# Down projection of a hybrid decoder step: the second of the two products with one weight block per step is computed third of seven instead of sixth

## The chip, the cores and the metric

The kernel runs on one core of a Trainium2 chip. The metric is the device time of one execution in microseconds, as the median of several runs. A core has PE for matmuls (its weight loads are listed as PEld), DVE and POOL for elementwise work, ACT for activations and copies, and SP, which here issues DMAs. PE adds up in eight PSUM banks.

## The reference, cut to what matters

The reference is one layer of a decoder: adaLN modulation, a gated DeltaNet branch and a sliding-window attention branch, and a gated feed-forward block, for 1024 prompt tokens and 8 single-token samples, all in float32. The change touches the last product, before the final norm:

```python
gc = _causal_dwconv(gate_ext, lp['ffn_conv_w'], L) + lp['ffn_conv_b']
x = x + gt2 * ((jax.nn.silu(gc) * up) @ lp['w_ffn_down'])
...
y_prompt = _rmsnorm(xp, final_norm_w)
y_sample = _rmsnorm(xs, final_norm_w)
```

The activations are (1032 tokens, 2816), `w_ffn_down` is (2816, 1024).

## The kernel before, in words

The kernel goes through the layer in stages; `second_half` (L1904) ends with `ffn_gate_up`, eleven times, and then `ffn_down` (L1726), which also does the final norm. The float32 operands of a product are split into a high and a low part, and `mm3` (L178, lines L180 to L182) makes three matmuls of each block product.

**Seven products.** `ffn_down` cuts activations, weights and output into two by two blocks and multiplies them with seven block products in place of eight, after the manner of Strassen. Each product runs over `G` = 11 steps of 128 rows, 77 steps in all. A step multiplies one activation block (128 x 516, from the scratch tensor `xd` in DRAM) with one weight block (128 x 512) into eight banks (two token halves by four column tiles), 24 matmuls in all. `made` says what a product's weight is made of: products 5 and 2 take one block of `w_ffn_down`, the other five take the sum or difference of two, which POOL computes (L1755).

**Chains.** `chains` gives the order of the products. The products of one tuple add into the same banks. After each product `take` (L1783) has ACT copy the eight banks to SBUF (L1786); PE's next product starts in the first bank once that is copied. The copies lie in a ring of eight slots and are added, times the gate, to the residual `x1` by `add_gated` on DVE (L1472, with L1476 and L1477 for the eight samples); `home` lists where each copy goes: two places, hence 16 additions, for products 5, 3, 1 and 2, and one place, hence 8, for 4 and 7. Product 6 is last, outside this loop, and is interleaved with the final norm.

**Loads.** `fetch` (L1742) issues the loads of a step on SP: a weight block (L1751), for a two-block product the other block into `ws` (L1754, three buffers), and the activation block (L1756). They land in one of five raw buffers: three of the pool `raw`, and two halves of `bmh0` (listed as `bmh`) for steps 3 and 4 of every five. `part` (L1759) splits a raw buffer: ACT writes the high part (L129), DVE the low part (L130); with the latter the raw buffer is free (a half of `bmh0` only together with the other half). The 13 places for split operands, `tags`, are used in turn, so step 39 lies in the same place as steps 0, 13 and 26; a place is free when PE has done the step that used it.

**Order.** `fetch_to` lets the splits run up to 13 steps ahead of PE, and loads four or five further. In the last six steps of each chain's last product it starts loads but no splits. Within these bounds a scheduler in the framework sets the order on each engine; each engine works through its own queue in that order.

Of the kernel before, what the change touches and what calls it, by code (L numbers as in the profile page):

```python
# [64 lines left out]
class Step:  # L65
# [1660 lines left out]
    def ffn_down(self, pool, psum):  # L1726
# [4 lines left out]
        made = {5: (2, (1, 1)), 3: (5, (0, 1), (1, 1), ALU.subtract), 4: (6, (1, 0), (0, 0), ALU.subtract),  # L1731
                7: (4, (1, 0), (1, 1), ALU.add), 1: (0, (0, 0), (1, 1), ALU.add), 2: (1, (0, 0)),
                6: (3, (0, 0), (0, 1), ALU.add)}
        chains = ((5, 3), (4, 7), (1,), (2,), (6,))
        home = {5: ((0, 0, -1), (1, 1, -1)), 3: ((1, 0, 1), (1, 1, 1)), 4: ((0, 1, 1),), 7: ((0, 0, 1),),
                1: ((0, 0, 1), (1, 1, 1)), 2: ((0, 1, 1), (1, 1, -1)), 6: ((1, 1, 1),)}
        steps = [(i, g) for c in chains for i in c for g in range(G)]
# [334 lines left out]
```

## Time and profile before

| what | value |
|---|---|
| median of 3 runs | 2083.78 us (2079.47 to 2090.38) |
| span of the profiled execution | 2084.4 us |
| PE busy over the span | 97% |
| HBM read and written | 212.93 MB, 62.51 MB |
| loads of `ffn_down`: `w_ffn_down` into `ws` | 55 of 256 KB |
| first copies after products 5, 3, 4 in this execution | 1862.8, 1895.17, 1933.32 us |

The profiled execution has no time listed beside its span. A row of the windows has the wall time of a stretch, then the busy time and number of instructions of each engine in it, then the clock granted to PE as a share of full speed, the mean busy share of the DMA engines, and GB/s. In a timeline a row starts with the start and duration in microseconds; the brackets at its end have the engine's idle time before it and what ended it. In the rows of waits, the total, the number and the longest follow the names.

### The profile page before, as it was taken

Reading aid. Unit: us, or ns where it says so; the run is one execution under the profiler, and the core shown is the slowest. Engines: PE = TensorE matmul, PEld = TensorE weight load, DVE = VectorE, ACT = ScalarE, POOL = GpSimd, SP = SyncE. Lnnn points to the kernel's source line nnn. Section 1 sums busy time; section 2 is a strip of 40 time slices with the busy share of each in tenths; the row PEclk is TensorE's granted clock in tenths of the full one; section 3 lists DMA queues with packets and bytes.
Section 4 is the critical chain, followed back from the end, with each engine's and each line's share of the span. In section 5 each row is a group of like instructions: output and inputs, shape, how many; then the busy total and the mean of one; then the engine's idle time right before and its main releaser. Section 6 shows DMA issues by size and latency. Waiting matters only on the chain.

```text
span 2084.4 us, 41297 instructions
## 1 busy us (share of the span) xinstructions
PE 2012.7 (97%) x16245; PEld 1910.2 (92%) x16245; DVE 1347.8 (65%) x2714; ACT 900.2 (43%) x2233; POOL 520.2 (25%) x594
## 2 busy tenths in 40 slices
PE   7999998999999999989989999999999999999897
PEld 4987877799999999989989999999999999999897
DVE  5755768473655647656544675578876776767756
ACT  4664545433344243432342542354444444534443
POOL 2000000121321221201111000005575466446421
PEclk9999999999999999999999999999999999999999
DMA  8256443331332322312275855323333333488862
GB/s 300 62 144 210 135 167 116 117 94 51 80 80 61 73 72 52 89 42 62 63 223 172 285 186 163 112 63 97 105 91 112 102 92 112 136 305 266 291 215 94
DMA packets 301887, 275.75 MB, mean 132 GB/s; under 512 B 59730, under 2 KB 248111, under 8 KB 301676
## 3 DMA queue, kind: packets, MB, share of 16 engines
q1 hardware_dynamic: 295642, 252.14, 39.6%
q0 software_dynamic: 5552, 20.37, 2.8%
q8 instruction: 127, 2.08, 0.4%
q14 instruction: 68, 0.56, 0.1%
q10 hardware_dynamic: 498, 0.61, 0.1%
HBM read 212.93 MB, written 62.51 MB: 132 GB/s over the span
## 4 chain that ended last, share of the span: by engine, by line
PE 83%; DVE 5%; DMA 5%; ACT 3%; issue 1%; SPq 1%; POOL 1%; DVEq 0%; POOLq 0%; ACTq 0%
PE mm L180 19%; PE mm L181 18%; PE mm L182 18%; PE wv L180 3%; PE wv L182 3%; PE wv L181 3%; PE wy L182 2%; PE wy L180 2%; PE wy L181 2%; PE pv L652 1%; PE pt L190 1%; PE tp L190 1%; DVE x L1472 1%; PE mm L264 1%; PE rc L954 1%
## 5 line engine op out<-in xcount | busy, mean ns | idle before, releaser
L180 PE MATMUL mm<-b1h,wh 128*128 128x384 f32 (+1 forms) x1520 | 496.9, 328 | 3.7 <-ACT gt L1294 1.6
L181 PE MATMUL mm<-b1l,wh 128*128 128x384 f32 (+1 forms) x1520 | 489.3, 323 | 0.0
L182 PE MATMUL mm<-b1h,wl 128*128 128x384 f32 (+1 forms) x1520 | 488.0, 323 | 0.3 <-DVE wl L130 0.3
L180 PEld LDWEIGHTS mm<-b1h,wh 128*128 128x128 f32 x1520 | 286.7, 189 | 12.4 <-issue 4.6
L181 PEld LDWEIGHTS mm<-b1l,wh 128*128 128x128 f32 x1520 | 287.1, 189 | 4.4 <-issue 3.1
L182 PEld LDWEIGHTS mm<-b1h,wl 128*128 128x128 f32 x1520 | 286.3, 189 | 3.9 <-issue 2.8
L129 ACT ACTIVATE wh<-raw 128x1024 fp32r<-128x1024 f32 x83 | 87.0, 1049 | 122.4 <-PE mm L181 70.2
L130 DVE TENSOR_TENSOR wl<-raw,wh 128x1024 fp32r<-128x1024 f32 x82 | 101.0, 1233 | 57.2 <-ACT wh L129 55.1
L181 PE MATMUL mm<-pk,w 128*128 128x260 f32 (+1 forms) x440 | 124.8, 284 | 1.1 <-DVE pk L130 1.1
L180 PE MATMUL mm<-pk,w 128*128 128x260 f32 (+1 forms) x440 | 124.8, 284 | 0.0
L182 PE MATMUL mm<-pk,w 128*128 128x260 f32 (+1 forms) x440 | 124.5, 283 | 0.0
L130 DVE TENSOR_TENSOR w<-ws,w 128x512 fp32r<-128x512 f32 x88 | 78.0, 886 | 36.9 <-ACT w L129 36.7
L1626 ACT COPY bml<-mm 128x256 f32<-128x256 f32 (+1 forms) x132 | 48.9, 371 | 100.6 <-PE mm L182 96.7
L180 PE MATMUL mm<-bmh,w 128*128 128x260 f32 (+1 forms) x320 | 90.3, 282 | 0.0
L182 PE MATMUL mm<-bmh,w 128*128 128x260 f32 (+1 forms) x320 | 90.1, 282 | 0.0
L1681 DVE SCALAR_TENSOR_TENSOR fa<-fz,fcw,fa 128x512 f32<-128x512 f32 x88 | 75.2, 874 | 18.2 <-ACT fa L1679 17.9
L180 PE MATMUL mm<-b2h,wh 128*128 128x384 f32 (+1 forms) x256 | 83.2, 328 | 2.9 <-ACT wh L129 2.8
L181 PEld LDWEIGHTS mm<-pk,w 128*128 128x128 f32 x440 | 83.2, 189 | 1.3 <-DVE pk L130 1.3
L181 PE MATMUL mm<-b2l,wh 128*128 128x384 f32 (+1 forms) x256 | 83.6, 327 | 0.4 <-DVE b2l L130 0.4
L180 PEld LDWEIGHTS mm<-pk,w 128*128 128x128 f32 x440 | 83.2, 189 | 0.2 <-ACT bml L1626 0.2
L182 PEld LDWEIGHTS mm<-pk,w 128*128 128x128 f32 x440 | 83.4, 190 | 0.0
L182 PE MATMUL mm<-b2h,wl 128*128 128x384 f32 (+1 forms) x256 | 82.8, 326 | 0.0
(645 smaller groups left out, 5886.2 us busy)
## 6 DMA issues: line engine op xcount, KB each, us to landing
raw<-in_w_in_dram SPq DMA_DIRECT2D x59, 512.0 KB
ws<-in_w_ffn_down_dram SPq DMA_DIRECT2D x55, 256.0 KB
raw<-xd SPq DMA_DIRECT2D x47, 258.0 KB
raw<-in_w_ffn_down_dram SPq DMA_DIRECT2D x47, 256.0 KB
raw<-in_w_ffn_gate_dram SPq DMA_DIRECT2D x22, 512.0 KB
raw<-in_w_ffn_up_dram SPq DMA_DIRECT2D x22, 512.0 KB
qst<-in_w_mod_dram SPq DMA_DIRECT2D x16, 512.0 KB
raw<-in_w_mod_dram SPq DMA_DIRECT2D x16, 512.0 KB
```

The costliest lines, as they stand in the source:

```text
L129: self.nc.scalar.activation(hi, x, AF.Copy)
L130: (eng or self.nc.vector).tensor_tensor(lo, x, hi.bitcast(F32), op=ALU.subtract)
L180: mm(ps, whi, xhi, start=first, stop=False, **kw)
L181: mm(ps, whi, xlo, start=False, stop=False, **kw)
L182: self.last_mm = mm(ps, wlo, xhi, start=False, stop=last, **kw).ins
L190: self.nc.tensor.transpose(out, in_, self.ident[:p, :p])
L264: nc.tensor.matmul(ps[32 * j:32 * j + 32], self.cT[:, k0 + j, :], ws[j // 2][:, j % 2, :], start=k0 == 0, stop=k0 > 0)
L652: nc.tensor.matmul(pv[64 * r:64 * r + 64], V[:, n - back, ch], ps[:, r::2, :], start=back == 0, stop=back == (n > 0))
L954: yield step(nc.tensor.matmul(ds, kd[:, n, :], s, start=True, stop=True))
L1472: nc.vector.scalar_tensor_tensor(x[:, :np_], ps[:, :np_], by[:, j, 8:9], x[:, :np_], op0=ALU.mult, op1=ALU.add)
L1626: self.last_copy = nc.scalar.copy(r[p, i], x[p])
L1681: nc.vector.scalar_tensor_tensor(ai[:, c:e], zi[:, j + c:j + e], col(j), ai[:, c:e], op0=ALU.mult, op1=ALU.add)
```

## The change

One line: product 2 moves from the fourth place in `chains` to the second. It stays a chain of its own.

```diff
@@ -1731,7 +1731,7 @@
         made = {5: (2, (1, 1)), 3: (5, (0, 1), (1, 1), ALU.subtract), 4: (6, (1, 0), (0, 0), ALU.subtract),
                 7: (4, (1, 0), (1, 1), ALU.add), 1: (0, (0, 0), (1, 1), ALU.add), 2: (1, (0, 0)),
                 6: (3, (0, 0), (0, 1), ALU.add)}
-        chains = ((5, 3), (4, 7), (1,), (2,), (6,))
+        chains = ((5, 3), (2,), (4, 7), (1,), (6,))
```

The order of the products is now 5, 3, 2, 4, 7, 1, 6. Steps 22 to 32 are product 2, 33 to 43 product 4, 44 to 54 product 7, 55 to 65 product 1; before, they were 4, 7, 1 and 2. Numbers behind the names in the rows below are the program's; the place's name gives the step.

POOL's queue at the end of product 3's subtractions, before: `raw_2848` belongs to step 21, the next rows to steps 22 to 25.

```order
L1755 TENSOR_TENSOR raw_2848_21399<-raw_2848_21399,ws_2849_21401 128x512
L1755 TENSOR_TENSOR raw_2851_21433<-raw_2851_21433,ws_2852_21435 128x512
L1755 TENSOR_TENSOR bmh0_2854_21475<-bmh0_2854_21475,ws_2855_21477 128x512
L1755 TENSOR_TENSOR bmh0_2854_21475<-bmh0_2854_21475,ws_2857_21510 128x512
L1755 TENSOR_TENSOR raw_2859_21541<-raw_2859_21541,ws_2860_21543 128x512
```

The same place in POOL's queue now: behind step 21 come steps 33 to 36.

```order
L1755 TENSOR_TENSOR raw_2848_21399<-raw_2848_21399,ws_2849_21401 128x512
L1755 TENSOR_TENSOR bmh0_2883_21839<-bmh0_2883_21839,ws_2884_21841 128x512
L1755 TENSOR_TENSOR bmh0_2883_21839<-bmh0_2883_21839,ws_2886_21849 128x512
L1755 TENSOR_TENSOR raw_2888_21880<-raw_2888_21880,ws_2889_21882 128x512
L1755 TENSOR_TENSOR raw_2891_21913<-raw_2891_21913,ws_2892_21915 128x512
```

For steps 22 to 32 POOL now has no instruction of this loop.

ACT's queue at the copies after product 4, before: `bmh3_2910` is the place of step 38, `bmh2_2912` of step 39, `bml0_2915` of step 40; product 4 ends with step 32.

```order
L129 ACTIVATE bmh3_2910_22022<-bmh0_2908_22016 128x1028
L129 ACTIVATE bmh2_2912_22056<-bmh0_2908_22016 128x1028
L1786 COPY bml3_2334_15602<-mm_2881_21849 128x256
L1786 COPY bml3_2334_15602<-wv_2882_21850 128x260
L129 ACTIVATE bml0_2915_22091<-raw_2913_22085 128x1028
L1786 COPY bml3_2334_15602<-wy_2883_21851 128x256
```

The copies after product 4 in ACT's queue now: `bmh3_2951` is the place of step 51, `bmh2_2955` of step 52; product 4 ends with step 43.

```order
L129 ACTIVATE bmh3_2951_22475<-raw_2949_22469 128x1028
L1786 COPY bml3_2334_15602<-mm_2911_22215 128x256
L1786 COPY bml3_2334_15602<-wv_2912_22216 128x260
L1786 COPY bml3_2334_15602<-wy_2913_22217 128x256
L1786 COPY bml3_2334_15602<-mm_2914_22218 128x260
L1786 COPY bml3_2334_15602<-wv_2915_22219 128x256
L129 ACTIVATE bmh2_2955_22513<-raw_2953_22507 128x1028
```

The first copy stood behind the split of the seventh step after product 4's last and now stands behind that of the eighth.

DVE's queue around the low parts of steps 38 and 39, before: the additions behind them are product 4's.

```order
L130 TENSOR_TENSOR bmh3_2910_22022<-bmh0_2908_22016,bmh3_2910_22022 128x1028
L130 TENSOR_TENSOR bmh2_2912_22056<-bmh0_2908_22016,bmh2_2912_22056 128x1028
L1472 SCALAR_TENSOR_TENSOR x1_0_2332_15597<-bml3_2334_15602,mT_125,x1_0_2332_15597 128x256
L1472 SCALAR_TENSOR_TENSOR x1_0_2332_15597<-bml3_2334_15602,mT_125,x1_0_2332_15597 128x252
L1476 TENSOR_TENSOR gtmp_2940_22378<-bml3_2334_15602,mT_125 128x8
```

The low part of step 38 in DVE's queue now, with the first of product 2's additions; sixteen L1472 rows in all stand ahead of the low part of step 39.

```order
L130 TENSOR_TENSOR bmh3_2899_21989<-bmh0_2897_21983,bmh3_2899_21989 128x1028
L1472 SCALAR_TENSOR_TENSOR x1_0_2332_15597<-bml3_2334_15602,mT_125,x1_0_2332_15597 128x256
L1472 SCALAR_TENSOR_TENSOR x1_4_2810_21062<-bml3_2334_15602,less_2807_21058,x1_4_2810_21062 128x256
L1472 SCALAR_TENSOR_TENSOR x1_0_2332_15597<-bml3_2334_15602,mT_125,x1_0_2332_15597 128x252
L1476 TENSOR_TENSOR gtmp_2937_22353<-bml3_2334_15602,mT_125 128x8
L1472 SCALAR_TENSOR_TENSOR x1_4_2810_21062<-bml3_2334_15602,less_2807_21058,x1_4_2810_21062 128x252
```

Both halves of `bmh0` that steps 38 and 39 use become free only after these additions.

## The prediction

> **What bounds the kernel now.** I read the page first, then PE's waits over the down projection, then windows around the one long wait, then the timelines of ACT, DVE, SP and POOL backwards from it. A step is one entry of `steps`; before the change product 5 is steps 0 to 10, product 3 is 11 to 21, product 4 is 22 to 32.
>
> ```profile
> span 2084.4 us, 41297 instructions
> ...
> PE 2012.7 (97%) x16245; PEld 1910.2 (92%) x16245; DVE 1347.8 (65%) x2714; ACT 900.2 (43%) x2233; POOL 520.2 (25%) x594
> ```
>
> PE is the bound and keeps all its matmuls, so time can only come from stretches where PE waits or runs slowly. PE's waits from 1780 us on:
>
> ```profile
> PE mm L180 <- ACT bml L1786: 5.6, 1, 5.6
> PE wv L190 <- DVE x L1477: 1.0, 1, 1.0
> ...
> PE wv L190 <- DVE raw L1896: 0.5, 1, 0.5
> ```
>
> One wait stands out; the others lie in the closing norm. Windows cut at it and at the closing norm (wall, then busy time and count of PE, PEld, DVE, ACT, POOL, then granted clock, DMA share, GB/s):
>
> ```profile
> 1928.16:1933.72 5.56, 0.00 (x1) 0.00 (x1) 3.28 (x3) 2.43 (x4) 3.56 (x3) 0.92 1.03 369
> 1933.72:1939.62 5.90, 5.90 (x27) 5.90 (x28) 5.87 (x7) 4.86 (x10) 3.52 (x4) 0.50 0.97 322
> 1939.62:1945.52 5.90, 5.90 (x52) 5.90 (x51) 5.90 (x11) 2.14 (x2) 2.69 (x3) 1.00 0.75 251
> 2045.42:2048.83 3.41, 1.82 (x14) 1.22 (x13) 3.33 (x10) 1.35 (x4) 0.89 (x2) 1.00 0.21 83
> 2048.83:2052.24 3.41, 3.41 (x18) 3.09 (x17) 2.64 (x15) 1.40 (x5) 1.10 (x2) 0.50 0.58 228
> ```
>
> The wait costs twice: 5.56 us of nothing, then 5.90 us at a clock of 0.50 (27 matmuls where the next 5.90 us hold 52), which is 2.95 us of lost work. Together 8.5 us: all that this place can give. Who made PE wait stands in ACT's timeline:
>
> ```profile
> 1928.87 1.06 ACT L129 ACTIVATE bmh<-bmh 128x1028 fp32r<-128x1028 f32 x1 [1.15 <-POOL bmh L1755]
> 1932.35 1.06 ACT L129 ACTIVATE bmh<-bmh 128x1028 fp32r<-128x1028 f32 x1 [2.42 <-POOL bmh L1755]
> 1933.32 0.35 ACT L1786 COPY bml<-mm 128x256 f32<-128x256 f32 x1
> ...
> 1936.40 1.11 ACT L129 ACTIVATE bml<-raw 128x1028 fp32r<-128x1028 f32 x1
> ```
>
> The L129 at 1932.35 is the split of step 39 (the room after step 38's, and so on: the one at 1936.40 is step 41's). It waits for POOL's subtraction, which waits for data; behind it in ACT's queue stand the copies L1786 that empty product 4's banks; and product 7 adds into those same banks, so PE stands until the first copy. The operands of step 39 itself are not needed for another six steps.
>
> Why was the data late? DMA had a hole shortly before (share 0.32), and the timelines of DVE and SP say why:
>
> ```profile
> 1910.00:1915.00 5.00, 5.00 (x45) 5.00 (x44) 5.00 (x8) 0.17 (x1) 0.00 (x0) 1.00 0.32 64
> ```
>
> ```profile
> 1896.77 2.70 DVE L1472 SCALAR_TENSOR_TENSOR x<-bml,mT,x 128x256 f32<-128x256 f32 x4
> ...
> 1902.25 1.22 DVE L130 TENSOR_TENSOR bml<-raw,bml 128x1028 fp32r<-128x1028 f32 x1
> ...
> 1909.83 1.22 DVE L130 TENSOR_TENSOR bml<-bmh,bml 128x1028 fp32r<-128x1028 f32 x1
> 1910.97 1.21 DVE L130 TENSOR_TENSOR bmh<-bmh,bmh 128x1028 fp32r<-128x1028 f32 x1
> ```
>
> ```profile
> 1905.43 1.77 SPq L1754 DMA_DIRECT2D ws<-in_w_ffn_down_dram  x2
> 1912.21 0.33 SPq L1751 DMA_DIRECT2D bmh<-in_w_ffn_down_dram  x1
> ...
> 1915.42 0.38 SPq L1754 DMA_DIRECT2D ws<-in_w_ffn_down_dram  x1
> ```
>
> Product 3's 16 additions (L1472) fill DVE from 1896.77 to 1909.83. Behind them wait the L130 of steps 28 and 29; these free the `bmh0` buffer, and only then, at 1912.21, can SP issue step 33. I call such a row of 16 additions a burst. From that issue to the end of step 41's split are 1937.5 - 1912.2 = 25.3 us.
>
> **The change part by part.** Matmuls, bytes, subtractions and additions keep their number; the 22 loads of product 2 pass in SP's queue ahead of the loads of products 4, 7 and 1, whose 33 subtractions move back by 11 steps in POOL's queue. What changes is what runs beside each burst. The same burst with and without POOL, and its DVE rows where POOL rests (now product 1's burst):
>
> ```profile
> 1896.77:1909.83 13.06, 13.06 (x112) 13.06 (x111) 13.06 (x24) 6.52 (x10) 7.15 (x5) 1.00 0.76 257
> 1997.42:2004.00 6.58, 6.58 (x58) 6.58 (x57) 6.58 (x20) 6.58 (x12) 0.00 (x0) 1.00 0.00 0
> ```
>
> ```profile
> 1997.42 1.68 DVE L1472 SCALAR_TENSOR_TENSOR x<-bml,mT,x 128x256 f32<-128x256 f32 x4 [10.33 <-ACT bml L1786]
> ...
> 2004.00 1.22 DVE L130 TENSOR_TENSOR pk<-raw,pk 128x1028 fp32r<-128x1028 f32 x1
> ```
>
> Beside five subtractions the burst takes 13.06 us, of which one L130 is 1.1 us: 11.9 us. Without POOL it takes 6.6 us. So a subtraction inside a burst costs it 5.3/5 = 1.06 us.
>
> Step 1, product 3's burst. Steps 22 to 32 now have one weight block, so POOL has nothing between steps 21 and 33, and the copies have no late split before them. The clock of PE is read from the last matmuls of steps 21 and 32 and from the first copy:
>
> ```profile
> 1896.42 0.28 PE L182 MATMUL nr<-pk 128*128 128x260 f32 x1
> ```
>
> ```profile
> 1927.88 0.28 PE L182 MATMUL nr<-pk 128*128 128x260 f32 x1
> 1933.72 0.58 PE L180 MATMUL mm<-pk 128*128 128x256 f32 x1 [5.56 <-ACT bml L1786]
> ```
>
> ```profile
> 1895.17 0.35 ACT L1786 COPY bml<-mm 128x256 f32<-128x256 f32 x1
> ```
>
> Eleven steps take 31.5 us, one 2.86. The first bank of a step has its last of three matmuls (0.12 us apart, 0.28 long) done 0.52 us into the step, 2.3 before its end, so a free copy starts near 1894.2 instead of 1895.17, and additions near 1894.6. Burst over: 1894.6 + 6.6 = 1901.2; two L130 at 1.14 us: step 33 issued at 1903.5, 8.7 us earlier than now. If the rest follows as it did, step 38's split ends at 1929.9 - 8.7 = 1921.2, well before the copies after product 2 (1925.7), ahead of which it now stands. That boundary costs nothing.
>
> Step 2, the new burst. Product 2's 16 additions now fall between the L130 of steps 38 and 39, where product 4's eight stood. They start near 1926.2. POOL's subtractions for steps 41 and 42 are
>
> ```profile
> 1934.59 1.46 POOL L1755 TENSOR_TENSOR raw<-raw,ws 128x512 f32<-128x512 f32 x1 [0.77 <-DMA raw<-in_w_ffn_down_dram]
> 1936.50 1.37 POOL L1755 TENSOR_TENSOR raw<-raw,ws 128x512 f32<-128x512 f32 x1 [0.46 <-DMA ws<-in_w_ffn_down_dram]
> ```
>
> and 8.7 us earlier they fall at 1925.9 and 1927.8, inside the burst. It takes 6.6 + 2 x 1.06 = 8.7 us, to 1934.9; step 39's L130 ends at 1936.1, and SP then issues step 43.
>
> Step 3, product 4's copies. They now stand behind the split of step 51, eight steps past 43, as 41 is past 33: 25.3 us, less one 256 KB block (0.7 us at 369 GB/s) because three blocks are fetched ahead instead of two. The split ends at 1936.1 + 24.6 = 1960.7, the first copy at 1961.0. PE finishes product 4 at 1928.0 + 31.5 = 1959.5. It waits 1.5 us. Bounds: a burst free of POOL, none; five subtractions in it, 1.5 + 3 x 1.06 = 4.7 us.
>
> Step 4, the slow clock behind the wait. In the closing norm PE idled 1.6 of 3.41 us, no single wait over 1.0 us, and the next 3.41 us ran at 0.50: 1.7 us lost. I charge the new wait that much. The Trainium skill (TensorE: Matmul & The Clock Gate, "What's actually happening") says that the clock halves after an idle window of about 3.4 us; by that rule a wait of 1.5 us costs no clock, and the forecast would be 1.7 us lower. The closing norm's row disagrees, since it was half busy there.
>
> Step 5, the closing stretch. Product 1's 16 additions stand where product 2's stood. They have four pairs of the small sample operations (L1476, L1477) instead of eight, and they touch columns 0 to 255, which the first transposes read. I count zero: at best the 1.5 us of L190 waits above go.
>
> Sum: 5.56 + 2.95 goes, 1.5 + 1.7 comes: -5.3 us. The profiled execution (2084.4) lies 0.6 us above the median 2083.78, so 2078.5 us against the median.
>
> **The rivals.** *The wait vanishes*: burst 2 meets no subtraction, or the loads run slightly faster; 2083.8 - 8.5 = 2075.3 us. For it: 1.5 us is all that is missing. Against it: DMA was saturated (1.03 and 0.97) while steps 34 to 41 came in.
>
> *A short wait leaves the clock alone*: 2078.5 - 1.7 = 2076.8 us. For it: the 5.56 us window reads 0.92, so the clock fell only in its last 0.9 us, some 4.7 us into the wait. Against it: the closing norm. The page's rule above is this rival.
>
> *The wait only moves*: burst 2 runs as dense with subtractions as product 3's did. Then 4.7 + 2.95 = 7.65 us stands against 8.5: 2082.9 us. For it: a 16-addition burst before the unpaused copies is just what is there now. Against it: the 8.7 us won at burst 1.
>
> *Slower*: the longer row of two-block steps, 33 to 76 without a light product between, loads more slowly than steps 33 to 41 did. The rows of steps 43 and 49:
>
> ```profile
> 1940.43 1.06 ACT L129 ACTIVATE pk<-bmh 128x1028 fp32r<-128x1028 f32 x1 [1.47 <-POOL bmh L1755]
> ...
> 1958.37 1.06 ACT L129 ACTIVATE pk<-bmh 128x1028 fp32r<-128x1028 f32 x1 [0.17 <-POOL bmh L1755]
> ```
>
> That is 17.94/6 = 2.99 us a step, where 33 to 41 took about 2.3. Eight steps at 0.68 more add 5.4 us; with a dense burst the wait is 4.7 + 5.4 = 10.1, and with 2.95 of slow clock 13.05 us against 8.5: 2088.3 us. It decides once step 51's split ends 4.1 us later than I have it (the old wait of 5.56 again). Against it: eight additions lay in that stretch, and none do in the new one.
>
> **How the numbers follow.** The shrunken wait has 0.42, the same with the clock left alone 0.12, the vanished one 0.20, the moved one 0.14, slower 0.12. The likeliest gives 2078.5 us. The range reaches from the vanished wait with the L190 waits gone too (2075.3 - 1.5 = 2073.8, taken as 2073.5) to just short of the slow rival, 2087. 0.5%, 10.4 us, is about what a measurement of this kernel can tell from no change. No rival alone passes it; the three runs scatter from 2079.47 to 2090.38, so part of the vanished wait falls beyond it (0.15 with what I have not seen), and part of the slow rival (0.07). The rest, 0.78, is within it.
>
> **What would show it.** Product 3's burst without subtractions at about 6.6 us; step 33 issued near 1903.5; no PE wait after product 2; a second burst of 7 to 9 us; one PE wait on L1786, now after product 4 near 1959.5 and under 5 us; at most one 3.4 us window at 0.50 behind it. I am wrong if PE waits after product 2, if the wait at product 4 exceeds 5.6 us, or if time moves in the closing stretch by more than 1.5 us.

## The result and the profile after

The changed kernel takes 2079.41 us in the median of 22 runs (2075.34 to 2088.55); the kernel before, run beside it, takes 2086.67 us (2077.44 to 2094.03, 22 runs). The ratio is 0.9971 with a 95% interval of 0.9959 to 0.9983, which is 6.0 us of 2086.67 (3.5 to 8.6); the two medians alone lie 7.3 us apart. The forecast was 5.3 us. One run of a later kernel (product 2 fifth) took 3917.54 us, for a cause that stays open, and is not in its ratio. The matmuls are all kept, as the page of the changed kernel shows:

```profile
span 2077.9 us, 41299 instructions
...
PE 2011.2 (97%) x16245; PEld 1908.0 (92%) x16245; DVE 1353.8 (65%) x2714; ACT 900.6 (43%) x2233; POOL 521.6 (25%) x594
```

The span is 6.5 us shorter. How far the change itself goes is better read from the first copy after product 5, ahead of which nothing is changed, to PE's last matmul. The windows of this stretch (wall, then busy time and count of PE, PEld, DVE, ACT, POOL, then clock, DMA share, GB/s), in the kernel before:

```profile
1862.80:2076.73 213.93, 205.45 (x1680) 203.21 (x1678) 154.16 (x239) 89.89 (x147) 84.83 (x57) 0.98 0.67 229
```

and in the changed kernel:

```profile
1864.23:2070.17 205.94, 201.34 (x1680) 199.29 (x1678) 157.08 (x239) 90.75 (x147) 86.67 (x57) 1.00 0.69 237
```

The same 1680 matmuls take 8.0 us less: PE idles 4.6 us instead of 8.5, and is busy 4.1 us less, because none of it runs at a lower clock. The stretch starts 1.4 us later in this execution, which has to be taken off where times are compared with the prediction. PE's waits from 1780 us on in the changed kernel:

```profile
PE mm L180 <- ACT bml L1786: 1.9, 1, 1.9
PE wy L190 <- ACT ws L1873: 1.0, 1, 1.0
PE wv L190 <- DVE raw L1896: 1.0, 1, 1.0
PE mm L181 <- DVE pk L130: 0.5, 1, 0.5
```

The wait of 5.6 us is now one of 1.9, still on L1786, and the closing norm's waits are the size they were. The stretches on which the prediction rested, as windows: the burst after product 3, the burst after product 2, and three of 3.41 us at the wait.

```profile
1896.10:1902.69 6.59, 6.59 (x57) 6.59 (x57) 6.59 (x20) 6.59 (x12) 0.00 (x0) 1.00 0.63 230
1927.59:1936.31 8.72, 8.72 (x75) 8.72 (x75) 8.72 (x20) 6.30 (x11) 2.77 (x2) 1.00 0.34 120
...
1958.71:1962.12 3.41, 2.34 (x20) 2.13 (x18) 1.14 (x2) 1.64 (x2) 2.80 (x3) 1.00 1.04 348
1962.12:1965.53 3.41, 2.62 (x22) 2.62 (x23) 3.40 (x3) 3.41 (x10) 2.45 (x2) 1.00 0.93 305
1965.53:1968.94 3.41, 3.41 (x31) 3.41 (x30) 3.41 (x7) 1.44 (x3) 1.86 (x2) 1.00 0.90 312
```

The first burst has no subtraction beside it (POOL 0.00) and takes 6.59 us; the second has two and takes 8.72. Behind the wait, which lies in the third and fourth row, the clock stays at 1.00. The second burst in DVE's timeline, with two of its additions that start ahead of a subtraction and two that start behind one:

```profile
1927.59 0.48 DVE L1472 SCALAR_TENSOR_TENSOR x<-bml,mT,x 128x256 f32<-128x256 f32 x1 [1.91 <-ACT bml L1786]
1927.99 1.52 DVE L1472 SCALAR_TENSOR_TENSOR x<-bml,less,x 128x256 f32<-128x256 f32 x1
1929.43 0.47 DVE L1472 SCALAR_TENSOR_TENSOR x<-bml,mT,x 128x252 f32<-128x252 f32 x1
...
1929.90 1.52 DVE L1472 SCALAR_TENSOR_TENSOR x<-bml,less,x 128x252 f32<-128x252 f32 x1
```

POOL's timeline beside them:

```profile
1927.78 1.45 POOL L1755 TENSOR_TENSOR raw<-raw,ws 128x512 f32<-128x512 f32 x1 [0.68 <-DMA ws<-in_w_ffn_down_dram]
1929.82 1.32 POOL L1755 TENSOR_TENSOR raw<-raw,ws 128x512 f32<-128x512 f32 x1 [0.59 <-DMA ws<-in_w_ffn_down_dram]
```

Each of the two additions that start behind a subtraction takes 1.05 us longer than its neighbours, and ends 0.28 us behind that subtraction's end. SP's issues of step 33 and of step 43, the first loads behind each burst:

```profile
1905.15 0.33 SPq L1751 DMA_DIRECT2D bmh<-in_w_ffn_down_dram  x1
...
1937.55 0.33 SPq L1751 DMA_DIRECT2D bmh<-in_w_ffn_down_dram  x1
```

And ACT's timeline at the wait: the split of step 51, and the copy that PE waits for right behind it.

```profile
1961.54 1.06 ACT L129 ACTIVATE bmh<-raw 128x1028 fp32r<-128x1028 f32 x1 [0.17 <-POOL raw L1755]
1962.51 0.35 ACT L1786 COPY bml<-mm 128x256 f32<-128x256 f32 x1
```

Product 4's last matmul ends at 1961.05; the copy starts 1.5 us after that and not before step 51's split.

### The profile page after: what moved, and what is told of

Same layout as the page of the kernel before. It is cut to its first block, busy times and chain, and to the rows that moved or that the text cites. A ratio compares the mean times of both kernels' runs of the same rounds, so it can differ in the third digit from the quotient of the medians.

```text
span 2077.9 us, 41299 instructions
## 1 busy us (share of the span) xinstructions
PE 2011.2 (97%) x16245; PEld 1908.0 (92%) x16245; DVE 1353.8 (65%) x2714; ACT 900.6 (43%) x2233; POOL 521.6 (25%) x594
## 4 chain that ended last, share of the span: by engine, by line
PE 79%; DMA 8%; DVE 6%; ACT 3%; issue 2%; POOL 1%; SPq 1%; DVEq 0%; POOLq 0%; ACTq 0%
PE mm L180 18%; PE mm L181 18%; PE mm L182 18%; PE wv L180 2%; PE wv L182 2%; PE wv L181 2%; DMA ws<-in_w_ffn_down_dram 2%; PE pv L652 1%; PE wy L180 1%; PE wy L181 1%; PE wy L182 1%; DMA raw<-in_w_swa_out_dram 1%; PE pt L190 1%; PE tp L190 1%; PE mm L264 1%
## 5 line engine op out<-in xcount | busy, mean ns | idle before, releaser
L129 ACT ACTIVATE wh<-raw 128x1024 fp32r<-128x1024 f32 x83 | 87.0, 1049 | 124.3 <-PE mm L181 72.9
L130 DVE TENSOR_TENSOR wl<-raw,wh 128x1024 fp32r<-128x1024 f32 x82 | 101.3, 1236 | 59.9 <-ACT wh L129 57.4
L130 DVE TENSOR_TENSOR w<-ws,w 128x512 fp32r<-128x512 f32 x88 | 77.8, 885 | 36.4 <-ACT w L129 36.2
```

The source lines that it names most:

```text
L129: self.nc.scalar.activation(hi, x, AF.Copy)
L130: (eng or self.nc.vector).tensor_tensor(lo, x, hi.bitcast(F32), op=ALU.subtract)
```

## The experiments

My theory: POOL's subtractions stretch the burst of additions after a product; the burst delays the low parts that free `bmh0`, so SP issues late, a split far ahead is late, and product 4's copies stand behind it. The rivals: it is the bytes that make the loads late (fewer are loaded now ahead of step 33); or only the place of the products counts, whatever their weight blocks. Beside that stands the price of the clock behind a wait, and the closing norm.

**The copies moved ahead of the late split, in the kernel before.**

```diff
-                    fetch_to(s + len(tags), i != c[-1] or g < G - 6)
+                    fetch_to(s + len(tags), i not in (4, c[-1]) or g < G - 6)
```

> The kernel before, with the splits paused in the last six steps of product 4 as well, so that product 4's copies stand right behind the split of step 38 and no longer behind that of step 39; the loads, subtractions and additions are as before. My theory (product 4's copies are late only because they stand behind the split of step 39, whose data POOL finishes at 1931 us): the wait of 5.6 us on L1786 shrinks, at most to the 2 us by which the split of step 38 (end 1929.9 in the kernel before) is behind product 4's last matmul (1928.2), no window at 0.50 follows, and the time falls by 6 to 8.5 us, to about 0.9965 of before. Rival (the loads as such are late, and the queue behind the copies only shows it): the wait returns within the next eleven steps as a wait of a matmul on L129 or L130, of 3 us or more, and the time falls by less than 3 us.

The wait on L1786, and ACT's timeline there, with the split of step 38:

```profile
PE mm L180 <- ACT bml L1786: 2.4, 1, 2.4
```

```profile
1931.84 1.06 ACT L129 ACTIVATE bmh<-bmh 128x1028 fp32r<-128x1028 f32 x1 [2.42 <-POOL bmh L1755]
1932.80 0.35 ACT L1786 COPY bml<-mm 128x256 f32<-128x256 f32 x1
```

With the same loads the wait falls from 5.6 to 2.4 us, no window at 0.50 follows, and no matmul waits for an L129 or L130 behind it. The stretch from product 5's first copy to PE's end takes 207.59 us, 6.3 less than before. The timed ratio is 0.9981 (0.9971 to 0.9992), a gain of 4.0 us (1.7 to 6.0): below the 6 to 8.5 that I expected, while the one profile lies inside that range. In the profiled execution the wait left PE 1.7 us of work in its window and cost no clock; whether it does in other executions, which would explain the lower timed gain, was not measured. The queue is shown as the cause of most of the wait; what is left is the split of step 38, which is late as well.

**No subtractions beside the burst after product 3, in the kernel before; all bytes loaded.**

```diff
-                nc.gpsimd.tensor_tensor(raw[:, n:], raw[:, n:], other, op=src[2])
+                22 <= s < 33 or nc.gpsimd.tensor_tensor(raw[:, n:], raw[:, n:], other, op=src[2])
```

> The kernel before without POOL's eleven subtractions L1755 of steps 22 to 32 (product 4 is then made with a wrong weight); both blocks are still loaded, so the DMA bytes are those of before. My theory (the burst of additions after product 3 is stretched by POOL's subtractions beside it): burst of 16 L1472 at 6.6 us instead of 13.06 (which held one L130), step 33 issued on SP at about 1904.5 us instead of 1912.2, the split of step 39 done before product 4 ends, the wait on L1786 under 1 us instead of 5.6, time 8.5 us less, about 0.996 of before. Rival (the 22 blocks loaded for these steps fill the DMA queues ahead of step 33): step 33 stays at 1912 or its data stays as late, and the wait stays at 4 us or more.

The burst as a window, the issue of step 33, and ACT's timeline at product 4's copies (the first row is the split of step 39):

```profile
1898.20:1904.70 6.50, 6.50 (x58) 6.50 (x57) 6.50 (x20) 4.42 (x8) 0.00 (x0) 1.00 1.05 398
```

```profile
1907.20 0.38 SPq L1751 DMA_DIRECT2D bmh<-in_w_ffn_down_dram  x1
```

```profile
1927.76 1.06 ACT L129 ACTIVATE bmh<-bmh 128x1028 fp32r<-128x1028 f32 x1 [2.44 <-POOL bmh L1755]
1928.72 0.35 ACT L1786 COPY bml<-mm 128x256 f32<-128x256 f32 x1
```

The burst takes 6.50 us although DMA ran at 1.05 and 398 GB/s beside it. The split of step 39 stands ahead of the copy as in the kernel before, but it is done in time, and PE has no wait on L1786. The ratio is 0.9960 (0.9946 to 0.9974), 8.3 us; 8.5 was expected. Step 33 was issued 2.7 us later than expected (1 us of it lies ahead of the stretch), which cost nothing. The bytes are out as the cause here.

**Another product in the third place.** The edit is shown against the kernel before.

```diff
-        chains = ((5, 3), (4, 7), (1,), (2,), (6,))
+        chains = ((5, 3), (1,), (4, 7), (2,), (6,))
```

> Product 1 instead of product 2 is third: a chain of its own, whose copies are not behind late splits, but with two weight blocks per step, so with subtractions. It tells two reasons for the gain of the change apart. My theory (the burst after product 3 must run beside steps without subtractions): the burst stays at 11 to 13 us, step 33 is issued near 1912 us, the copies after product 1 wait 1 to 3 us for the split of step 38, and the second burst, also beside subtractions, makes the split of step 51 end near 1968 us, 7 us behind product 4's last matmul: waits of 7 to 10 us in all, so the time is 0 to 5 us above before. Rival (what helps is only that a product with paused copies stands between product 3's burst and the unpaused copies of product 4, whatever its weight blocks): a wait of 2 us after product 4 and the time of the changed kernel, 6 us below before.

The waits on L1786, the two bursts as windows (the first holds one L130 of 1.2 us), and the issue of step 33:

```profile
PE mm L180 <- ACT bml L1786: 7.1, 2, 3.6
```

```profile
1895.10:1909.21 14.11, 14.11 (x121) 14.11 (x120) 14.11 (x23) 7.39 (x10) 7.98 (x6) 1.00 0.77 265
1932.42:1942.01 9.59, 9.59 (x71) 9.59 (x70) 9.59 (x20) 4.57 (x6) 3.75 (x3) 0.83 0.49 176
```

```profile
1911.59 0.33 SPq L1751 DMA_DIRECT2D bmh<-in_w_ffn_down_dram  x1
```

Two waits of 3.6 us stand where the changed kernel has one of 1.9, and the ratio is 1.0011 (0.9999 to 1.0024). So a product with paused copies in the third place does not help by itself: it must leave POOL idle beside the burst. The place rival is refuted.

**Product 2 fifth, product 1 sixth.** The edit is shown against the kernel before.

```diff
-        chains = ((5, 3), (4, 7), (1,), (2,), (6,))
+        chains = ((5, 3), (4, 7), (2,), (1,), (6,))
```

> Only the order of the products after 4 and 7 changes: product 2 is fifth and product 1 sixth. Up to product 7 every queue is as before, so both theories keep the wait of 5.6 us after product 4, with windows at 0.50 behind it. The closing norm now stands behind product 1's additions, as in the changed kernel. If the 1.4 to 1.7 us that the closing stretch gained there come from these additions, the window at 0.50 in the closing norm is missing here too and the time is about 1.6 us below before (0.9992). If it was only how PE's short waits lay in the clock's windows of 3.41 us in that one execution, the closing norm has waits of L190 of the same kind and size as before, and the time is that of before within 1 us.

The ratio is 1.0003 (0.9991 to 1.0016). The profile is of another execution of this kernel (2089.75 us):

> Product 2 fifth and product 1 sixth once more, for a profile of an undisturbed execution. Product 4's wait stays at 5.6 us (within 0.5) with one or two windows at 0.50 behind it, since every queue up to product 7 is as in the kernel before. In the closing norm, which now stands behind product 1's additions: if these are what shortens it, PE waits there under 2.5 us in all, as in the changed kernel, against 2.7 in the kernel before and 2.7 to 3.5 in the runs with product 2's additions there; if not, the same 2.7 us or more.

Its waits:

```profile
PE mm L180 <- ACT bml L1786: 5.8, 1, 5.8
PE wv L190 <- DVE raw L1896: 1.0, 1, 1.0
PE wy L190 <- ACT ws L1873: 1.0, 1, 1.0
PE mm L181 <- DVE pk L130: 0.4, 1, 0.4
```

Product 4's wait is back, and the closing waits are 2.4 us in all. That fits the shorter closing stretch that I asked about, but the waits do not settle it: with product 1's additions ahead of the closing norm they are 2.5 (changed kernel), 2.4 (here), and 3.4, 2.8 and 2.6 in runs below; with product 2's they are 2.7 in the kernel before, 3.2, 3.5 and 2.7. The two sets overlap, and the time shows no gain, though its interval (1.9 us down to 3.3 us up) would hide one of 1 us. The row at 0.50 in the closing norm of the kernel before is missing in all three other runs with product 2's additions there, so it belonged to that one execution.

**The pause in the changed kernel.** The edit is the first one's.

> The changed kernel, with the splits paused in the last six steps of product 4 as well: its copies stand right behind the split of step 49 (end 1957.86 us in the changed kernel), 3 us ahead of product 4's last matmul. My theory (the 1.9 us that are left are the same queue as before, with a later split in front): no wait on L1786 at all, and the time is 2 to 3 us below the changed kernel, 0.996 of before; since the lateness of the loads is not touched, operands could only run short behind it if they were within 2 us of being late, and I expect no new wait over 0.5 us. Rival (the loads are the limit): a wait of a matmul on L129 or L130 of about 2 us in the steps after 44, and the time of the changed kernel.

All of PE's waits from 1780 us on:

```profile
PE wv L190 <- DVE x L1472: 1.4, 1, 1.4
PE wv L190 <- DVE raw L1896: 1.0, 1, 1.0
PE wy L190 <- ACT ws L1873: 1.0, 1, 1.0
```

The wait on L1786 is gone and no wait on L129 or L130 takes its place. A wait of 1.4 us is new, against my expectation; it is the closing norm that waits for product 1's burst, which took 10.8 us here and 9.4 in the changed kernel, beside subtractions in both. The ratio to the kernel before is 0.9951 (0.9932 to 0.9969), 2076.08 us in the median, the lowest of all kernels that compute everything. Against the changed kernel the stretch is 1.4 us shorter (204.59 to 205.94 us); the two ratios' intervals overlap between 0.9959 and 0.9969, so this second gain is not settled by the times alone.

**Two subtractions less beside the second burst, in the changed kernel.**

```diff
-                nc.gpsimd.tensor_tensor(raw[:, n:], raw[:, n:], other, op=src[2])
+                s in (41, 42) or nc.gpsimd.tensor_tensor(raw[:, n:], raw[:, n:], other, op=src[2])
```

> The changed kernel without POOL's subtractions L1755 of steps 41 and 42 alone, the two that overlap the second burst (product 4's weight is then wrong in two steps); their loads stay. My theory (each subtraction inside a burst costs it about 1.06 us, and the burst's end moves everything behind it): the second burst takes 6.6 us instead of 8.7, step 43 is issued near 1935.5 us instead of 1937.55, the split of step 51 ends near 1960.5 instead of 1962.6, the wait on L1786 falls from 1.9 us to under 0.3, and the time is 2 us below the changed kernel, 0.996 of before. Rival (the rate of the loads from step 43 to 51 sets the wait, the burst does not): step 51's split moves by less than 1 us and the wait stays over 1 us.

This execution is about 7 us later by this place, so I count from product 2's first copy, at 1934.49 us (1927.18 in the changed kernel). The second burst, the issue of step 43, and ACT at product 4's copies:

```profile
1934.92:1941.53 6.61, 6.61 (x58) 6.61 (x57) 6.61 (x20) 6.29 (x11) 0.00 (x0) 1.00 0.37 121
```

```profile
1942.77 0.33 SPq L1751 DMA_DIRECT2D bmh<-in_w_ffn_down_dram  x1
```

```profile
1966.49 1.06 ACT L129 ACTIVATE bmh<-raw 128x1028 fp32r<-128x1028 f32 x1 [1.18 <-POOL raw L1755]
1967.47 0.35 ACT L1786 COPY bml<-mm 128x256 f32<-128x256 f32 x1
```

The burst takes 6.61 us instead of 8.72; step 43 is issued 8.28 us behind that copy instead of 10.37; step 51's split ends 33.1 us behind it instead of 35.4; PE does not wait. Two subtractions cost 2.1 us at the burst, and the same 2.1 at the issue and 2.3 at the split. The stretch takes 204.00 us, 1.9 less than in the changed kernel; the ratio to the kernel before is 0.9959 (0.9945 to 0.9973), whose interval overlaps the changed kernel's, so it is the trace and not the time that shows this gain.

**The bytes put back, in the changed kernel.**

```diff
+            elif i == 2:
+                nc.sync.dma_start(self.t(self.pw, [P, 512], "ws", bufs=3), src[0])
```

> The changed kernel with the eleven loads of 256 KB that product 2's steps save put back as unused loads: each of the steps 22 to 32 loads its weight block into the buffer of the second block as well, and nothing reads it. POOL has no more to do than in the changed kernel. My theory (the subtractions beside the burst, not the bytes, made the loads late): the burst after product 3 stays at 6.6 us, step 33 is issued within 1.5 us of where the changed kernel has it (10.1 us after product 3's first copy begins), the wait after product 4 stays between 1 and 3 us, and the time is within 1.5 us of the changed kernel (about 0.997 of before). Rival (the change works by the fewer bytes ahead of step 33): step 33 or the splits behind it come 2 us or more later, the wait after product 4 is 4 us or more, and at least half of the gain is gone.

Windows of the burst after product 3, of the 3.41 us that hold the wait after product 4, and of the next 3.41:

```profile
1902.54:1908.94 6.40, 6.40 (x56) 6.40 (x56) 6.40 (x18) 4.97 (x8) 0.00 (x0) 1.00 1.03 383
...
1965.50:1968.91 3.41, 1.50 (x12) 1.42 (x12) 2.92 (x2) 3.23 (x8) 2.47 (x2) 1.00 0.92 320
1968.91:1972.32 3.41, 3.41 (x18) 3.41 (x17) 3.41 (x7) 2.47 (x5) 1.87 (x2) 0.50 1.03 328
```

The burst is as short as without the bytes (two of the small sample operations fall behind it here), step 33 is issued 10.2 us behind product 3's first copy (9.5 in the changed kernel by its trace, not the 10.1 of the expectation), and the wait is 1.9 us again. The ratio is 0.9975 (0.9965 to 0.9985): the gain stays. This wait of 1.9 us is followed by half the clock (18 matmuls where the changed kernel's row has 31), though the changed kernel's wait of 1.9 us was not.

**Waits made on purpose.** In the changed kernel the first bank is copied several times (11, 12, 13, 14 after products 3, 2, 7, 1; then 11 each), with the other copies behind it:

```diff
-            self.took = nc.scalar.copy(r, ps)
+            with ExitStack() as late:
+                if i in (3, 2, 7, 1) and (p, j) != (0, 0):
+                    late.enter_context(self.tc.issue_after(self.took.ins))
+                for _ in range({3: 11, 2: 12, 7: 13, 1: 14}.get(i, 1) if (p, j) == (0, 0) else 1):
+                    self.took = nc.scalar.copy(r, ps)
```

> The changed kernel with waits of PE made on purpose: after products 3, 2, 7 and 1 the first bank is copied 11, 12, 13 and 14 times (0.35 us each) in place of once, and the other copies follow; the output is the same. The first copy can start 2.3 us ahead of the product's last matmul, so PE should wait about 1.6, 2.0, 2.3 and 2.7 us there, besides the 1.9 us after product 4. It tells what the clock does behind a wait. The step of my prediction (any wait of about 1.5 us costs the next 3.41 us half the clock): a row at 0.50 behind each of the five. The rule that only an idle window of about 3.4 us halves the clock: none. My theory now (windows of 3.41 us run freely, and one with more than about half of it idle, 1.7 us, halves the next): it depends on how each wait lies across the windows; none behind the 1.6, and behind the longer ones only where one window holds 1.7 us or more of the wait, so two or three of the four.

The waits came out at 2.03, 2.43, 2.81 and 3.19 us. The first two, cut at the clock's windows:

```profile
1897.14:1900.55 3.41, 1.47 (x13) 1.25 (x11) 0.00 (x0) 3.16 (x10) 0.00 (x0) 1.00 0.98 369
1900.55:1903.96 3.41, 3.33 (x15) 3.33 (x16) 3.35 (x11) 3.41 (x10) 0.00 (x0) 0.50 0.06 20
1931.27:1934.68 3.41, 2.59 (x22) 2.38 (x20) 0.00 (x0) 3.01 (x9) 2.39 (x2) 1.00 0.64 219
1934.68:1938.09 3.41, 1.80 (x15) 1.80 (x16) 1.82 (x6) 3.32 (x12) 0.17 (x1) 1.00 0.35 107
1938.09:1941.50 3.41, 3.41 (x30) 3.41 (x30) 3.41 (x11) 3.41 (x5) 0.00 (x0) 1.00 0.00 0
```

The shorter wait, nearly all in one window, costs the clock; the longer one, split 0.8 to 1.6, does not. The waits of 2.81 and 3.19 us put 2.81 and 2.27 us into one window, and both cost it.

> Waits of PE made on purpose once more, this time four alike: the first bank is copied 11 times after products 3, 2, 7 and 1, which gave 2.03 us of wait where it was tried, about what the changed kernel has after product 4 (1.9). It tells whether the changed kernel's wait left the clock alone by luck. My theory (a free-running window of 3.41 us with more than about half of it idle halves the clock in the next): a wait of 2.03 us costs the clock where at least about 1.75 us of it lie in one window, so about six or seven times in ten; two or three of the four here. Rival (a wait under a whole window costs nothing, the case before was chance): none. Rival (any such wait costs, the step of my prediction): all four.

> The same kernel in a second execution, in which the windows lie elsewhere: again two or three of the four waits cost the clock by my theory, and not necessarily the same ones; none or all four by the rivals. The bound between a wait that costs and one that does not should come out between 1.70 and 1.95 us of idle time in one window.

Of the eight made waits (1.99 to 2.04 us) only one cost the clock, fewer than I expected; but each went by its window: that one, behind product 7 in the first execution, left PE 1.40 us of work in a window, and in the second execution the same wait left 2.27 in one and 2.55 in the next. In the second execution, product 2's made wait and product 4's own, each with the window behind it:

```profile
1928.72:1932.13 3.41, 1.66 (x14) 1.45 (x13) 0.00 (x0) 3.13 (x9) 1.94 (x2) 1.00 0.53 181
1932.13:1935.54 3.41, 3.12 (x26) 3.12 (x27) 3.14 (x10) 3.41 (x10) 0.61 (x1) 1.00 0.46 139
1962.85:1966.27 3.42, 1.38 (x11) 1.17 (x10) 1.72 (x2) 2.65 (x5) 2.94 (x3) 1.00 0.98 332
1966.27:1969.68 3.41, 3.41 (x17) 3.41 (x17) 3.41 (x3) 2.74 (x9) 2.04 (x2) 0.50 0.95 279
```

Both waits are 2.04 us long. The first leaves PE 1.66 us busy in its window and the clock stays; the second leaves 1.38 and it halves. In these three runs, the run with the bytes put back and the pause in the kernel before, every window at clock 1.00 that held such a wait and 1.50 us or less of PE's work was followed by 0.50, and none with 1.66 us or more.

## Why the prediction was right, and where it was not

*The chain of causes* held. The copies behind a late split made PE wait (the pause alone takes 3.2 of 5.6 us off), and the split was late because subtractions stretched the burst (without them, and with all bytes, the wait is gone).

*Step 1.* The burst was forecast at 6.6 us and took 6.59. With the 1.4 us by which the execution is later, step 33 was forecast at 1904.9 and issued at 1905.15. Step 38's split ended at 1924.42 instead of 1922.6, since the loads behind step 33 ran slower than before; it still stood well ahead of the copies at 1927.18, and nothing waited, as said.

*Step 2.* 8.7 us with two subtractions at 1.06 us each; 8.72 was measured, and 6.61 with these two left out.

*Step 3.* The wait was forecast at 1.5 us and is 1.9: step 51's split ended at 1962.60, where 1962.1 stands for the forecast.

*Step 4 failed.* It read "I charge the new wait that much", 1.7 us of slow clock for any such wait. In the profiled execution the wait cost no clock at all; in the run with the bytes put back it cost the whole 1.7. What decides is how the wait lies across windows of 3.41 us that run on regardless of it. The changed kernel's wait put 1.07 us into one and 0.79 into the next. A wait costs the clock only where enough of it falls into one window: 1.75 us without work was seen to cost none, 1.91 to cost. If the bound is the first, I estimate the chance of a wait of 1.87 us as (3.41 - 1.87 + 2 x 0.12) / 3.41, a little over a half; if it is the second, there is none, as the wait is shorter. So the mean charge lies between nothing and 0.9 us instead of 1.7. Step 4 took its price from the row of the closing norm, and that is the one row that does not fit these bounds (see the last section).

*The rival of the clock left alone* described the profiled execution, but its reason is refuted: PE had 1.38 to 1.50 us of work in windows that were followed by 0.50. The rule in the Trainium skill (TensorE: Matmul & The Clock Gate, "What's actually happening") that the gate halves after an idle window, read as one without any work, is too mild by these rows; that its window is free-running and 3413 ns long agrees with them.

*Step 5* counted zero for the closing stretch. In the two profiles it moved by 1.7 us, more than the 1.5 that the prediction names as a sign of being wrong. As windows from the last matmul ahead of product 6 to PE's end, before and changed:

```profile
2030.99:2076.73 45.74, 42.81 (x339) 40.79 (x338) 31.48 (x82) 16.85 (x45) 9.20 (x10) 0.96 0.25 96
...
2026.12:2070.17 44.05, 41.32 (x339) 39.48 (x338) 31.63 (x76) 16.87 (x45) 10.37 (x10) 1.00 0.29 110
```

PE is busy 1.5 us less there, and the row at 0.50 in the kernel before belonged to that one execution. But it is not the whole of it: without such a row the stretch took 45.2, 45.5 and 44.1 us in the other runs with product 2's additions ahead of it, and 43.6 to 44.8 in four runs with product 1's (those with a made wait in this stretch left out). About 1 us of gain from product 1's place is possible; these few executions overlap and the time of product 2 fifth does not show it, so it stays open.

*The sum.* From the traces: the wait 5.56 to 1.87 is -3.7, the slow clock behind it -2.95, and 0 to 0.9 is to be charged in the mean: -6.6 to -5.7 us. The forecast had -5.3, and the timed ratio gives -6.0 (-8.6 to -3.5). The profiled stretch gives -8.0, of which 1.7 lies in the closing stretch; the 6.3 left stand against 6.6 from the wait and its clock. That the prediction came so close is in part luck: step 3 was 0.4 us too low, step 4 0.8 to 1.7 too high, and what step 5 put at zero is open. The prediction also took 10.4 us as about what a measurement of this kernel can tell from no change; with 22 runs of each the interval is 5 us wide, and 6.0 us was clear of zero.

*The other rivals.* The wait did not vanish, since burst 2 did meet subtractions; with these two gone it does. It did not just move. And the loads from step 43 on were slower than forecast by 0.5 us, not by the 4.1 that would have decided for *slower*: from the issue of step 43 to the end of step 51's split are 25.1 us, 24.6 were forecast.

## What to carry to other kernels

A wait on a copy may have its cause in another engine's queue: go back from the copy to what stands ahead of it, then to the data of that, and then to what kept the buffer busy. Where two engines slow each other, give the long row of one a neighbour that leaves the other idle; and keep urgent copies out from behind work for steps far ahead, which by itself took 3.2 of 5.6 us off the wait here, in one profile. Price a short wait of PE by its own length, and the slow clock behind it by a chance, not by a single profile.

## What the runs showed of the hardware

An addition of DVE on 128x256 f32 took 0.47 us alone and 1.52 where it started behind a subtraction of POOL; two subtractions taken away shortened a burst by 2.1 us. The Trainium skill (SBUF — State Buffer, "SBUF: two separate sides") tells of one port pair that an operation of DVE with two inputs in SBUF and one of GpSimd take exclusively, the other blocking meanwhile; the 1.05 us that an addition loses to a subtraction of 1.32 or 1.45 us agrees. DMA at 383 to 398 GB/s beside the same burst did not lengthen it (6.40 and 6.50 us).

The clock: in the runs named above, 1.50 us or less of matmuls in a window of 3.41 us was followed by 0.50, 1.66 or more was not, and the windows lay elsewhere against the same waits in a second execution. In a window at 0.50 behind a wait, 2.67 us of work or less (2.41 in the kernel before) was followed by a second one at 0.50, and 3.33 or more by 1.00, so one wait can cost one slow window or two. One row does not fit the first bound: in the closing norm of the kernel before, a window with 1.82 us of work, 1.52 of it transposes, was followed by 0.50. Transposes may count for less than matmuls there, but they count for something: in the run with product 1 third a window with 2.47 us of transposes and nothing else was followed by 1.00. This was not tried by itself.
